# A hybrid encoder layer on one core: its interleaving planned with other durations, late issue of operations that wait for transfers, and the inverse's rows fetched by a transfer

## The chip, the cores and the metric

The kernel runs on one core of a Trainium2 chip. The metric is the device time of one execution in microseconds (us), a median of three runs; lower is better.

## What is computed

One layer over 1024 frames of width 1024, all in float32. Three groups of heads mix over time, a dense SwiGLU network follows, RMS norms stand before each and at the end:

```
h  = rmsnorm(x, ln1_g);  p = h @ w_in
ym = mlstm_group(pm, ...)     # 4 heads of 64, chunks of 64 frames in the reference
yr = retention_group(pr)      # 6 heads, chunkwise
yw = rwkv7_group(pw, ...)     # 6 heads, a recurrence per frame:
#   S = S * w_t - (S kk_t) (kk_t a_t)^T + v_t k_t^T ;  y_t = S r_t
x  = x + concat(ym, yr, yw) @ w_out
h  = rmsnorm(x, ln2_g)
x  = x + (silu(h @ w_gate) * (h @ w_up)) @ w_down       # D_FF 2816
return rmsnorm(x, lnf_g)
```

## The kernel before

Products of full precision are made of three products of rounded parts: each operand is split into a high part (`split_hi`, ScalarE, L90) and a low part (`split_lo`, VectorE, L93), and TensorE adds high x high, high x low and low x high. These triples are the dense work: L119 to L121 (512 columns), L729 to L731 (256 columns, token-major), L1171 to L1173 (first feed-forward layer), L1364 to L1366 (down-projection).

**The mixer** (up to some 760 us) is a set of generators, each a stream of its own: `rwkv_chain`, `rwkv_inverse`, the preparation of the RWKV heads, the output `rwkv_out`, `attention` (mLSTM and retention) and, last, `fillers` and `out_proj`, which bring the dense work. `weave` interleaves them as the program is written: it keeps a clock, each stream says with `yield cost, wait` how long its piece takes TensorE and how long its results take, and `yield "name"` waits for a `signal`. The stream whose time has come writes its next piece. Each engine executes its instructions in the order that comes out of this, and each engine waits at its own head. A stream that is in `sharing` holds the two accumulators until its tile is done.

**The RWKV recurrence** is taken in chunks of 64 frames. `rwkv_chain_pair` runs 16 steps, one after the other, for each of three pairs of heads, 48 in all. A step is: product of X and E (L581), copy to `pm` on ScalarE (L583), products L586 and L590, two copies to X on ScalarE (L592, L593), products L597 and L600, then the new state: X on VectorE (L607), its copy `st` on GpSimd (L609). Between these pieces `weave` puts pieces of other streams.

Each half of a pair needs the inverse of triangular matrices, six inverses in all (numbered 1 to 6 here). Gram products (L460) leave them in E; four small stores write them to `ab_d` in DRAM; one load brings them back as `MN`, each matrix in a partition, in four copies (L507). ScalarE copies the rows that each partition works on into `R` (L509, four copies). VectorE inverts by substitution in about 45 small operations (L514 to L522), GpSimd sets the diagonal of R (L527, four clearings to 1, the first of which needs only that R be there), R goes to `r_d` in DRAM and from there into E (L532). VectorE transposes a half of it (L535, tile `tq`), and two sets of small products on TensorE (L540, L546) complete the 64x64 inverse.

**Behind the mixer** `out_tile(1, d)` makes the second half of the output projection, in parts of six dense products; between parts, `between` steps `second_norm(0)`: `rms_stats` sums the squares (L159, of `sqa2`, which GpSimd has added up at L1049) and takes the root (L162), `rms_expand` spreads it over columns (L166). `second_half(d)` prepares operands on ScalarE, VectorE and GpSimd. Then comes the first feed-forward layer; its activations go to `a_dram` in DRAM, but for the tiles listed in `DIRECT`, which stay in SBUF. Before the down-projection `take` loads them back four tiles at a time (`rg`, two buffers) and splits them.

SyncE issues every transfer, in program order.

Of the kernel before, what the change touches and what calls it, by code (L numbers as in the profile page):

```python
# [19 lines left out]
P = 128  # L20
# [34 lines left out]
def trunk_kernel(ctx: ExitStack, tc: tile.TileContext, a: dict, out: bass.AP):  # L55
# [60 lines left out]
    def three(ps, w, xh, xl, ks=range(KT)):  # L116
        for k in ks:
# [3 lines left out]
            PE.matmul(ps, lhsT=lo, rhs=xh[:, k, :], start=False, stop=(k == KT - 1))  # L121
# [4 lines left out]
    clock, events = [0.0], {}  # L126
# [4 lines left out]
    def weave(gens, sharing):  # L131
        live = [[0.0, None, g] for g in gens + sharing]
        holder = None
        while live:
# [4 lines left out]
            got = next(s[2], None)  # L139
# [13 lines left out]
    PART = 6 * 0.214  # L153
# [36 lines left out]
    LAT = 0.93  # L190
    CHAIN, INV, ATT, NORM, MIX = 3.51, 20.16, 3.09, 3.26, 1.28
# [189 lines left out]
    def rwkv_half(i, h, r, k, v):  # L381
# [18 lines left out]
        yield 0.9, 3.0  # L400
# [32 lines left out]
        yield 2.6, 5.0  # L433
# [20 lines left out]
        yield 0.9, 5.5  # L454
# [20 lines left out]
        yield 3.4, 3.0  # L475
# [9 lines left out]
        yield 0.9, 1.0  # L485
# [14 lines left out]
    def rwkv_inverse():  # L500
        for i in range(3):
            for h in range(2):
# [5 lines left out]
                for g in range(4):  # L508
                    S.copy(out=R[lane(g)], in_=MN[lane(g), g::4, :])  # L509
                yield 0.0, 8.0  # L510
# [3 lines left out]
                V.tensor_tensor(tv, mf[:, 34:34 + 15 * 66:66].unsqueeze(2).broadcast_to([P, 15, 32]), MN[:, 2:31:2], ALU.mult)  # L514
# [18 lines left out]
                yield 0.0, 7.5  # L533
                for q in range(2):
                    V.transpose(out=T11[blk(q, 0)], in_=E[blk(q, 0), :, q, col(0)])  # L535
# [15 lines left out]
                yield 0.9, 3.0  # L551
# [5 lines left out]
    def rwkv_chain_pair(i):  # L557
        st = None
        for h in range(2):
# [3 lines left out]
            for c in range(8):  # L563
# [20 lines left out]
                yield 0.2, LAT  # L584
# [9 lines left out]
                yield 0.2, LAT  # L594
# [24 lines left out]
                yield 0.4, CHAIN  # L619
# [4 lines left out]
    def rwkv_out():  # L624
# [3 lines left out]
        for i in range(3):  # L628
            for h in range(2):
                yield f"prep{i}{h}"  # L630
                for b in range(2):
# [6 lines left out]
                    G.tensor_tensor(add, add, ga, ALU.mult)  # L638
# [11 lines left out]
                    signal(f"out{n}", 0.5)  # L650
                    V.tensor_tensor(gl, gl, pt, ALU.mult)
# [7 lines left out]
                    yield 0.9, 0.0  # L659
# [47 lines left out]
    def tok_proj(g, ts=range(KT)):  # L707
# [16 lines left out]
        for t in ts:  # L724
            ps = acc_tile()
            o = ps[:, 0:n]
            h, sl = chunk_of(t)
            for k in range(KT):
                PE.matmul(o, lhsT=xh[h][:, k, sl], rhs=w[k][0], start=(k == 0), stop=False)  # L729
                PE.matmul(o, lhsT=xh[h][:, k, sl], rhs=w[k][1], start=False, stop=False)  # L730
                PE.matmul(o, lhsT=xl[h][:, k, sl], rhs=w[k][0], start=False, stop=(k == KT - 1))  # L731
                if k == 3:
                    yield 12 * 0.42e-3 * n, 0.0, True
# [4 lines left out]
            elif g in (2, 3, 4):  # L738
                v4, o4 = (z.rearrange("p (h x d) -> p h x d", x=2, d=32) for z in (vt, o))
                cs = rot[:, t, :].rearrange("p (w x d) -> p w x d", w=2, x=2)  # L740
                b4 = etmp(256, "vb").rearrange("p (h x d) -> p h x d", x=2, d=32)
                V.scalar_tensor_tensor(vt.rearrange("p (h d) -> p h d", d=64), in0=o.rearrange("p (h d) -> p h d", d=64),
                                       scalar=rstd[:, t:t + 1], in1=rot[:, t:t + 1, 0:64].broadcast_to([P, 4, 64]),
# [17 lines left out]
            cost = 12 * 0.42e-3 * n  # L761
# [7 lines left out]

    rot = at.tile([P, KT, P], F32, name="rot", tag="rot")  # L770
    SY.dma_start(out=rot, in_=a["rot"])
# [360 lines left out]
    with ExitStack() as ph3:  # L1132
# [174 lines left out]
        def take(h, g, parts=None):  # L1307
# [6 lines left out]
            for f in range(gs.start, gs.stop, 4)[parts or slice(None)]:  # L1314
# [10 lines left out]
                for z in range(0, n, 2):  # L1325
# [3 lines left out]
                    for y in range(o, o + 2):  # L1329
                        ah[h, gs.start + y] = hi[:, y, :], lo[:, y, :]  # L1330
# [232 lines left out]
```

## Time and profile before

| | |
|---|---|
| runs | 1519.3, 1505.03, 1511.74 us; median 1511.74 |
| the profiled execution | 1521.67 us, span 1519.9 us, mean TensorE clock 0.952 |
| TensorE busy | 1425.6 us (94%), 8434 products |
| VectorE, ScalarE, GpSimd busy | 59%, 37%, 29% |
| transfers | 164.55 MB, 33.5% of 16 engines |
| chain that ended last | TensorE 53%, VectorE 3%, GpSimd 2%, transfers 2% |

The profile gives each instruction's start and length, the idle time of its engine before it, and behind an arrow what ended that idle time. The granted clock is a share of full speed. Products are pipelined, so the length of one (0.39 us for 512 columns) is more than the distance to the next.

### The profile page before, as it was taken

The page shows a single profiled execution, that of the slowest core. Times are in us where ns is not written, and L with a number is a line of the kernel's source. Part 1 is how long each engine was busy: PE and PEld are TensorE (multiplying, and loading weights), DVE is VectorE, ACT ScalarE, POOL GpSimd, SP SyncE. Part 2 cuts the span into 40 slices and gives each one's busy share as a digit, 9 for nine tenths or more (in the row PEclk, how much of TensorE's full clock was granted, in tenths as well). Part 3 has the DMA queues.
Part 4 walks back from the last instruction along what each step waited for, and adds up shares of the span by engine and source line. Part 5 has one row for each costly group of instructions (what it writes and reads, how often), then busy time and mean ns, then how long its engine had stood idle before and what let it go on. Part 6 is the DMA issues. An engine that isn't in the chain of part 4 may idle for free.

```text
span 1519.9 us, 23085 instructions
## 1 busy us (share of the span) xinstructions
PE 1425.6 (94%) x8434; PEld 1161.3 (76%) x8434; DVE 892.4 (59%) x1762; ACT 556.2 (37%) x1202; POOL 437.9 (29%) x539
## 2 busy tenths in 40 slices
PE   7998799789998998999998999999999998999996
PEld 5777577777777887887777887888888886887886
DVE  6457567458847756645468555555555565347434
ACT  6353334333432133244456333333333344224222
POOL 3211013234424333333545433344444420000000
PEclk9999999999978889899999999999999999999998
DMA  5142122334422244354632222222222247337333
GB/s 209 43 136 66 50 80 74 83 89 112 122 59 68 85 129 124 106 161 142 220 112 85 96 83 83 72 73 78 83 84 83 83 168 255 93 95 238 98 97 111
DMA packets 122269, 164.55 MB, mean 108 GB/s; under 512 B 38028, under 2 KB 70956, under 8 KB 120876
## 3 DMA queue, kind: packets, MB, share of 16 engines
q1 hardware_dynamic: 122156, 163.08, 33.5%
q8 instruction: 66, 1.08, 0.3%
q14 instruction: 47, 0.39, 0.1%
HBM read 124.75 MB, written 38.29 MB: 107 GB/s over the span
## 4 chain that ended last, share of the span: by engine, by line
PE 53%; DVE 3%; POOL 2%; DMA 2%; issue 1%; ACT 0%; POOLq 0%; DVEq 0%; SPq 0%; ACTq 0%
PE acc L1171 5%; PE acc L1172 5%; PE acc L1173 5%; PE chain L1365 5%; PE chain L1364 5%; PE chain L1366 5%; PE misc L1172 4%; PE misc L1171 4%; PE misc L1173 4%; PE acc L119 2%; PE acc L121 2%; PE acc L120 2%; DVE act L93 1%; PE acc L729 1%; PE acc L731 1%
## 5 line engine op out<-in xcount | busy, mean ns | idle before, releaser
L93 DVE TENSOR_TENSOR wlo<-wraw,whi 128x512 fp32r<-128x512 f32 (+1 forms) x210 | 147.9, 707 | 138.3 <-ACT whi L90 137.1
L90 ACT ACTIVATE whi<-wraw 128x512 fp32r<-128x512 f32 (+1 forms) x210 | 128.1, 612 | 226.3 <-PE chain L1365 117.9
L729 PE MATMUL acc<-whi,act 128*128 128x256 f32 (+1 forms) x512 | 161.3, 318 | 4.4 <-ACT whi L90 3.4
L90 ACT ACTIVATE whi<-rg 128x512 fp32r<-128x512 f32 x128 | 79.8, 631 | 228.7 <-POOL rg L1232 90.0
L730 PE MATMUL acc<-wlo,act 128*128 128x256 f32 (+1 forms) x512 | 155.4, 305 | 5.2 <-DVE wlo L93 5.2
L119 PE MATMUL acc<-act,whi 128*128 128x512 f32 x352 | 152.3, 433 | 7.0 <-ACT whi L90 6.2
L93 DVE TENSOR_TENSOR wlo<-rg,whi 128x512 fp32r<-128x512 f32 x128 | 93.1, 728 | 108.1 <-ACT whi L90 105.9
L731 PE MATMUL acc<-whi,act 128*128 128x256 f32 (+1 forms) x512 | 153.0, 300 | 0.0
L1364 PE MATMUL chain<-act,whi 128*128 128x512 f32 (+1 forms) x374 | 144.3, 386 | 4.0 <-ACT act L90 4.0
L120 PE MATMUL acc<-act,whi 128*128 128x512 f32 x352 | 145.5, 413 | 1.5 <-DVE act L252 1.5
L121 PE MATMUL acc<-act,wlo 128*128 128x512 f32 x352 | 145.7, 414 | 1.1 <-DVE wlo L93 1.1
L1365 PE MATMUL chain<-act,whi 128*128 128x512 f32 (+1 forms) x374 | 144.0, 385 | 0.5 <-DVE act L93 0.5
L1366 PE MATMUL chain<-act,wlo 128*128 128x512 f32 (+1 forms) x374 | 143.8, 384 | 0.0
L1171 PE MATMUL acc<-act,whi 128*128 128x512 f32 x352 | 139.3, 396 | 3.4 <-ACT pre L1432 2.7
L1173 PE MATMUL acc<-act,wlo 128*128 128x512 f32 x352 | 138.8, 394 | 0.0
L1172 PE MATMUL acc<-act,whi 128*128 128x512 f32 x352 | 138.5, 394 | 0.0
L729 PEld LDWEIGHTS acc<-whi,act 128*128 128x128 f32 x512 | 104.3, 205 | 12.1 <-ACT whi L90 3.9
L730 PEld LDWEIGHTS acc<-wlo,act 128*128 128x128 f32 x512 | 105.0, 206 | 9.2 <-DVE wlo L93 6.7
L731 PEld LDWEIGHTS acc<-whi,act 128*128 128x128 f32 x512 | 105.2, 206 | 1.0
L1172 PE MATMUL misc<-act,whi 128*128 128x512 f32 x264 | 104.1, 394 | 0.0
L1171 PE MATMUL misc<-act,whi 128*128 128x512 f32 x264 | 104.0, 394 | 0.0
L1173 PE MATMUL misc<-act,wlo 128*128 128x512 f32 x264 | 103.8, 393 | 0.0
(327 smaller groups left out, 2835.9 us busy)
## 6 DMA issues: line engine op xcount, KB each, us to landing
wraw<-in_w_down SPq DMA_DIRECT2D x85, 256.0 KB, 2.7
rg<-in_w_gate SPq DMA_DIRECT2D x22, 512.0 KB, 4.9
rg<-in_w_up SPq DMA_DIRECT2D x22, 512.0 KB, 5.0
a_dram<-work SPq DMA_DIRECT2D x41, 256.0 KB, 2.2
wraw<-in_w_tm SPq DMA_DIRECT2D x40, 256.0 KB, 3.0
rg<-a_dram SPq DMA_DIRECT2D x10, 1024.0 KB, 6.1
v_dram<-vt SPq DMA_DIRECT2D x64, 128.0 KB, 1.9
wraw<-in_w_out SPq DMA_DIRECT2D x32, 256.0 KB, 3.2
```

The source lines that it names most:

```text
L90: S.activation(hi, src, AF.Copy, scale=scale)
L93: (eng or V).tensor_tensor(lo, src, hi.bitcast(F32), ALU.subtract)
L119: PE.matmul(ps, lhsT=hi, rhs=xh[:, k, :], start=(k == 0), stop=False)
L729: PE.matmul(o, lhsT=xh[h][:, k, sl], rhs=w[k][0], start=(k == 0), stop=False)
L730: PE.matmul(o, lhsT=xh[h][:, k, sl], rhs=w[k][1], start=False, stop=False)
L731: PE.matmul(o, lhsT=xl[h][:, k, sl], rhs=w[k][0], start=False, stop=(k == KT - 1))
L1171: PE.matmul(ps, lhsT=hi, rhs=hi_x[:, k, :], start=(start and k == 0), stop=False, skip_group_check=True)
L1172: PE.matmul(ps, lhsT=hi, rhs=lo_x[:, k, :], start=False, stop=False, skip_group_check=True)
L1173: PE.matmul(ps, lhsT=lo, rhs=hi_x[:, k, :], start=False, stop=(stop and k == 3), skip_group_check=True)
L1364: PE.matmul(ps, lhsT=hi, rhs=hi_a[:, sl], start=(f == 0), stop=False)
L1365: PE.matmul(ps, lhsT=hi, rhs=lo_a[:, sl], start=False, stop=False)
L1366: PE.matmul(ps, lhsT=lo, rhs=hi_a[:, sl], start=False, stop=(f == FT - 1))
```

## The change

It has these parts:

- `weave` starts at 10.0 and uses other costs and waits throughout. The pieces of streams that do not share the accumulators are issued behind the last dense product written (`issue_after(dense[0])`).
- `late(eng)` issues an operation behind the last instruction that was written for its engine, wherever the scheduler would have put it. It is used for the inverse's first operation and its transposes, GpSimd's product in `rwkv_out`, the split of `yw`, and the mLSTM weights, which are now made in a function of their own.
- R is loaded from `ab_d` by a transfer of 1024 rows of 128 bytes, behind that of MN; the four copies are gone.
- The rotary table, one load of 512 KB before, is loaded in 24 tiles of 64 KB, two buffers, where it is used.
- `second_norm` sums three parts later for the first half, and four parts, not two, lie between sum and expansion. `second_half(7)` is issued behind ScalarE's first copy to `pre`.
- Four tiles of activations stay in SBUF, not two, and the load of tiles 16 to 19 brings only the two that do not.

```diff
-    clock, events = [0.0], {}
+    clock, events = [10.0], {}
+    def late(eng):
+        return tc.issue_after(next(i for i in reversed(nc.cur_bb.bb.instructions) if i.engine == eng.engine))
+    dense = [None]
...
-            got = next(s[2], None)
+            with nullcontext() if s[2] in sharing or dense[0] is None else tc.issue_after(dense[0]):
+                got = next(s[2], None)
...
-    PART = 6 * 0.214
+    PART, TOK = 6 * 0.23, 12 * 0.47e-3
-    LAT = 0.93
-    CHAIN, INV, ATT, NORM, MIX = 3.51, 20.16, 3.09, 3.26, 1.28
+    LAT, CHAIN, INV, ATT, NORM, MIX = (1.2, 1.6), 3.4, 28.0, 4.0, 4.0, 1.6
...
                 SY.dma_start(out=MN, in_=ab_d.rearrange("b q c s t -> (b q c) (s t)").unsqueeze(0).broadcast_to([4, 32, 1024]))
-                for g in range(4):
-                    S.copy(out=R[lane(g)], in_=MN[lane(g), g::4, :])
-                yield 0.0, 8.0
+                SY.dma_start(out=R, in_=ab_d.rearrange("b q c (j g) t -> g (b q c) j t", g=4))
+                yield 0.0, 11.0
...
-                V.tensor_tensor(tv, mf[:, 34:34 + 15 * 66:66].unsqueeze(2).broadcast_to([P, 15, 32]), MN[:, 2:31:2], ALU.mult)
+                with late(V):
+                    V.tensor_tensor(tv, mf[:, 34:34 + 15 * 66:66].unsqueeze(2).broadcast_to([P, 15, 32]), MN[:, 2:31:2], ALU.mult)
...
-                yield 0.0, 7.5
+                yield 0.0, 9.0
                 for q in range(2):
-                    V.transpose(out=T11[blk(q, 0)], in_=E[blk(q, 0), :, q, col(0)])
+                    with late(V):
+                        V.transpose(out=T11[blk(q, 0)], in_=E[blk(q, 0), :, q, col(0)])
...
                 S.copy(out=pm, in_=chn[:, 0:64])
-                yield 0.2, LAT
+                yield 0.4, LAT[0]
...
                 S.copy(out=X[64:128, c, 1, :], in_=chn[64:128, 64:128])
-                yield 0.2, LAT
+                yield 0.45, LAT[1]
...
-                    G.tensor_tensor(add, add, ga, ALU.mult)
...
                     signal(f"out{n}", 0.5)
+                    with late(G):
+                        G.tensor_tensor(add, add, ga, ALU.mult)
...
+            if g in (2, 3, 4):
+                rot = at.tile([P, P], F32, name="rot", tag="rot", bufs=2)
+                SY.dma_start(out=rot, in_=a["rot"][:, t, :])
...
-                cost = 12 * 0.42e-3 * n
+                cost = TOK * n
...
-    rot = at.tile([P, KT, P], F32, name="rot", tag="rot")
-    SY.dma_start(out=rot, in_=a["rot"])
...
+    def mlstm_weights(c, ws):
+        for q, w in enumerate(ws):
...
+                yield 0.0, 3.0
+                with late(S):
+                    split_hi(yh[:, 5 + i], yw)
...
         rms_stats(const, [sqa2[h]], 4, f"b{h}", rs)
-        yield
-        yield
+        for _ in range(4):
+            yield
...
-        DIRECT = (FT - 2, FT - 1)
+        DIRECT = range(FT - 4, FT)
...
-                n = min(4, gs.stop - f)
+                here = [y for y in range(f, min(f + 4, gs.stop)) if h == 0 and y in DIRECT]
+                n = min(4, gs.stop - f) - len(here)
...
-        between = chain(second_norm(0), first_half())
+        between = chain(second_norm(0, 4), first_half())
...
-        second_half(KT - 1)
...
-                S.copy(out=pre[j, m], in_=ps[m])
+                copy = S.copy(out=pre[j, m], in_=ps[m])
+                if j == m == 0:
+                    with tc.issue_after(copy.ins):
+                        second_half(KT - 1)
```

What this does to the order of instructions is shown at three places; the line numbers of the new kernel differ from those of the old.

On VectorE, around the start of inverse 6 in the kernel before (`rt<-MN` is the inverse's first operation, `X<-st,dl,chain` the chain's new state, `vt` and `wlo` belong to the dense streams):

```order
L758 SCALAR_TENSOR_TENSOR vt<-acc,rstd_x,vt 128x256
L514 TENSOR_TENSOR rt<-MN 128x480
L515 TENSOR_TENSOR MN<-MN,rt 128x15x32
L519 TENSOR_TENSOR rt<-R,MN 128x60
L758 SCALAR_TENSOR_TENSOR vt<-acc,rstd_x,vt 128x256
L522 TENSOR_TENSOR R<-R,rt 128x30
L93 TENSOR_TENSOR wlo<-wraw,whi 128x512
L522 TENSOR_TENSOR R<-R,rt 128x30
L607 SCALAR_TENSOR_TENSOR X<-st,dl,chain 64x64
```

The same place in the changed kernel:

```order
L762 TENSOR_TENSOR vt<-acc,rdec 128x256
L520 TENSOR_TENSOR rt<-MN 128x480
L93 TENSOR_TENSOR wlo<-wraw,whi 128x512
L521 TENSOR_TENSOR MN<-MN,rt 128x15x32
L614 SCALAR_TENSOR_TENSOR X<-st,dl,chain 64x64
L525 TENSOR_TENSOR rt<-R,MN 128x60
L614 SCALAR_TENSOR_TENSOR X<-st,dl,chain 64x64
L528 TENSOR_TENSOR R<-R,rt 128x30
```

The first half of X stands three instructions behind the first operation on MN, where it stood seven behind, and the second half stands behind the first operation that reads R.

On ScalarE at the same inverse, in the kernel before (`pm` and `X` are the chain's copies):

```order
L583 COPY pm<-chain 128x64
L509 COPY R<-MN 32x256 x4
L755 ACTIVATE vt<-acc,rhalf 128x256
L592 COPY X<-chain 64x64
L593 COPY X<-chain 64x64
```

In the changed kernel, with tile numbers, at the step of the chain that follows inverse 6's Gram products:

```order
L590 COPY pm_6579<-chain_6578 128x64
L90 ACTIVATE whi_6765<-wraw_6747 128x512
L90 ACTIVATE whi_6773<-wraw_6749 128x512
L599 COPY X_4912<-chain_6578 64x64
L600 COPY X_4912<-chain_6578 64x64
```

The four copies of R stood between the chain's copies; nothing of the inverse stands there now.

On TensorE where the token-major tiles of `fillers` end and the output projection begins, in the changed kernel (L588 to L607 are a chain step, L547 and L553 the two sets of products of inverse 6, L953 a transpose of the retention, L119 to L121 and L742 dense products; `E_6203` is the tile whose inverse is number 6):

```order
L742 MATMUL acc_7223<-whi_7082,act_109 128x256
L588 MATMUL chain_7292<-X_4912,E_5055 64x64 x2
L119 MATMUL acc_7527<-act_6245,whi_7519 128x512
L120 MATMUL acc_7527<-act_6246,whi_7519 128x512
L121 MATMUL acc_7527<-act_6245,wlo_7520 128x512
L593 MATMUL chain_7292<-pm_7293,E_5055 64x64 x2
L597 MATMUL chain_7292<-st_7203,E_5055 64x64 x2
...
L604 MATMUL chain_7292<-X_4912,E_5055 64x64 x2
...
L547 MATMUL misc_7255<-tq_7122,E_6203 32x32 x15
...
L588 MATMUL chain_7379<-X_6089,E_6203 64x64 x2
L121 MATMUL acc_7527<-act_6245,wlo_7520 128x512
L553 MATMUL misc_7255<-E_6203,tq_7123 32x32 x16
```

In the kernel before, the second set of inverse 6 and the first step that uses that inverse stand there (L729 and L731 are token-major dense products):

```order
L546 MATMUL misc_6889<-E_5951,tq_6670 32x32 x16
...
L731 MATMUL acc_7006<-whi_6778,act_109 128x256
L581 MATMUL chain_7021<-X_5793,E_5951 64x64 x2
L729 MATMUL acc_7006<-whi_6786,act_108 128x256
L730 MATMUL acc_7006<-wlo_6787,act_108 128x256
L731 MATMUL acc_7006<-whi_6786,act_109 128x256
```

The last eight steps of the chain and the end of inverse 6 stood among the token-major tiles, 26 rows apart; they now begin where these tiles end, side by side.

More of the change, by code (lines that the diff above doesn't have):

```diff
@@ L1 @@
 import math
-from contextlib import ExitStack
+from contextlib import ExitStack, nullcontext
 from itertools import chain
@@ L730, in tok_proj @@
                 PE.matmul(o, lhsT=xh[h][:, k, sl], rhs=w[k][1], start=False, stop=False)
[L731 removed]
+                dense[0] = PE.matmul(o, lhsT=xl[h][:, k, sl], rhs=w[k][0], start=False, stop=(k == KT - 1)).ins
                 if k == 3:
[L733 removed]
+                    yield TOK * n, 0.0, True
             vt = etmp(256, "vt")
@@ L1098, in attention, with weigh @@
     def attention():
-        mlstm = ("mlstm", 2.6, mlstm_load, mlstm_chunk, mlstm_finish, None)
-        ret = ("ret", 4.0, ret_load, ret_chunk, ret_finish, ret_store)
+        def weigh(t, args):
+            if len(args) == 4:
+                with late(G):
+                    mlstm_weights(t, args[-1])
+        mlstm = ("mlstm", 4.2, mlstm_load, mlstm_chunk, mlstm_finish, None)
+        ret = ("ret", 5.0, ret_load, ret_chunk, ret_finish, ret_store)
         for (name, cost, load, chunk, finish, store), start, ts in (
@@ L1106, in attention @@
             yield 0.0, 6.0
+            weigh(ts.start, args)
+            yield 0.0, 2.0
             for t in ts:
@@ L1314, in take @@
             for f in range(gs.start, gs.stop, 4)[parts or slice(None)]:
-                n = min(4, gs.stop - f)
-                if h == 0 and f in DIRECT:
-                    for y in range(f, f + n):
-                        o = y - gs.start
-                        split_hi(hi[:, o, :], direct[y])
-                        split_lo(lo[:, o, :], direct[y], hi[:, o, :])
-                        ah[h, y] = hi[:, o, :], lo[:, o, :]
-                    continue
-                r = sb.tile([P, 4, HF], F32, name="rg", tag="rg", bufs=2)
-                SY.dma_start(out=r[:, 0:n, :], in_=a_dram[h][:, f:f + n, :])
-                for z in range(0, n, 2):
-                    o = f - gs.start + z
-                    split_hi(hi[:, o:o + 2, :], r[:, z:z + 2, :])
-                    split_lo(lo[:, o:o + 2, :], r[:, z:z + 2, :], hi[:, o:o + 2, :])
-                    for y in range(o, o + 2):
-                        ah[h, gs.start + y] = hi[:, y, :], lo[:, y, :]
+                here = [y for y in range(f, min(f + 4, gs.stop)) if h == 0 and y in DIRECT]
+                n = min(4, gs.stop - f) - len(here)
+                if n:
+                    r = sb.tile([P, 4, HF], F32, name="rg", tag="rg", bufs=2)
+                    SY.dma_start(out=r[:, 0:n, :], in_=a_dram[h][:, f:f + n, :])
+                parts = [(f + z, 2, r[:, z:z + 2, :]) for z in range(0, n, 2)] + [(y, 1, direct[y].unsqueeze(1)) for y in here]
+                for y, m, src in parts:
+                    o = slice(y - gs.start, y - gs.start + m)
+                    split_hi(hi[:, o, :], src)
+                    split_lo(lo[:, o, :], src, hi[:, o, :])
+                    for z in range(m):
+                        ah[h, y + z] = hi[:, o.start + z, :], lo[:, o.start + z, :]
         x3 = {}
```

29 lines of the change are left out of this document (15 added, 14 removed).

## The prediction

> **What bounds the kernel now.** I read the page's first, second and fourth parts, then stretches of the span, then what TensorE waited for.
>
> ```profile
> PE 1425.6 (94%) x8434; PEld 1161.3 (76%) x8434; DVE 892.4 (59%) x1762; ACT 556.2 (37%) x1202; POOL 437.9 (29%) x539
> PE 53%; DVE 3%; POOL 2%; DMA 2%; issue 1%; ACT 0%; POOLq 0%; DVEq 0%; SPq 0%; ACTq 0%
> 0.00:750.00 750.00, 681.55 (x5172) 557.56 (x5173) 473.90 (x1178) 283.78 (x750) 230.48 (x396) 0.92 0.34 106
> 750.00:820.00 70.00, 64.56 (x274) 52.16 (x274) 50.30 (x59) 39.54 (x67) 38.19 (x26) 0.95 0.42 140
> 820.00:1240.00 420.00, 416.55 (x1802) 336.61 (x1802) 232.91 (x320) 143.50 (x247) 162.62 (x114) 1.00 0.24 83
> 1240.00:1265.00 25.00, 20.50 (x81) 15.86 (x80) 18.99 (x24) 12.38 (x17) 3.77 (x2) 0.89 0.72 253
> ```
>
> In the stretches the first number after the bounds is the length, the second TensorE's busy time, and the number third from the end the granted clock. TensorE bounds the whole, but not evenly. From 820 to 1240 us it is busy for 416.55 of 420 us at full clock: nothing is to be had there, and 416.55 / 1802 gives the price of a dense product of 512 columns, 0.23 us. Up to 750 us, the mixer, it stands idle for 750 - 681.55 = 68 us, and a mean clock of 0.92 costs another 0.08 x 750 = 60 us. The change works on this stretch, on the 70 us behind it (5.4 us idle, 3.5 us of clock) and on the start of the down-projection (4.5 us idle, 0.11 x 25 = 2.8 us of clock). That is some 145 us that an edit of the order can reach at all. The waits name the places:
>
> ```profile
> PE misc L540 <- DVE tq L535: 10.5, 3, 7.7
> PE chain L597 <- ACT X L593: 7.8, 3, 6.0
> PE chain L586 <- ACT pm L583: 7.6, 5, 2.0
> PE chain L1364 <- ACT act L90: 4.0, 1, 4.0
> PE misc L159 <- POOL sqa L1049: 3.8, 1, 3.8
> PE acc L729 <- ACT whi L90: 3.4, 2, 3.0
> PE acc L1171 <- ACT pre L1432: 2.7, 2, 1.6
> PE misc L166 <- POOL rs L162: 1.6, 1, 1.6
> ```
>
> (Total, times, longest.) The waits put down to ScalarE, `ACT`, come from no slow ScalarE, as the longest of them shows, first in order of time and then as two stretches:
>
> ```profile
> 584.40 0.53 SPq L507 DMA_DIRECT2D MN<-ab_d  x1
> 588.49 0.33 PE L586 MATMUL chain<-pm,E 64*64 64x64 f32 x4
> 594.03 1.65 ACT L509 COPY R<-MN 32x256 f32<-32x256 f32 x4 [6.80 <-DMA MN<-ab_d]
> 594.03 0.66 DVE L514 TENSOR_TENSOR rt<-MN 128x480 f32<-128x480 f32 x1 [5.89 <-DMA MN<-ab_d]
> 596.08 0.19 ACT L592 COPY X<-chain 64x64 f32<-64x64 f32 x1
> 596.56 0.48 PE L597 MATMUL chain<-X,E 128*64 128x64 f32 x4 [6.02 <-ACT X L593]
> 590.20:593.70 3.50, 0.34 (x3) 0.14 (x2) 0.00 (x0) 0.00 (x0) 0.00 (x0) 1.00 0.22 71
> 593.70:600.50 6.80, 3.94 (x23) 3.83 (x24) 5.29 (x15) 4.93 (x14) 1.52 (x4) 0.50 0.18 60
> ```
>
> The inverse's copy out of MN stands at the head of ScalarE's queue 6.80 us before MN lands; the chain's copy of X, whose input was there from 588.8 us, stands behind it, and TensorE in its own queue behind that. Then the clock falls to 0.50 for 6.8 us, which costs 3.4 us more. So a stall of 6 us costs 9.4.
>
> **The change part by part.** *R by transfer, the inverse's first operation and transposes later.* Six times four copies leave ScalarE; nothing of the inverse then waits for MN there. The stalls behind such a copy are the three of L597 (7.8), the longest of L586 (2.0) and of L729 (3.0): 12.8 us. The 7.69 us of L540 are the same thing on VectorE:
>
> ```profile
> 161.24 0.66 DVE L514 TENSOR_TENSOR rt<-MN 128x480 f32<-128x480 f32 x1 [7.81 <-DMA E<-r_d]
> 162.54 0.44 DVE L535 STREAM_TRANSPOSE tq<-E 32x256 f32<-32x256 f32 x1
> 163.12 0.28 PE L540 MATMUL misc<-tq,E 32*32 32x32 f32 x2 [7.69 <-DVE tq L535]
> ```
>
> The first inverse's transposes stand behind the second's first operation, which waits for MN. In the new order the pair of transposes stands ahead of it. Together 20.5 us at most. I leave 3 us for what follows: the wait for MN stays on VectorE, and now the chain's X update stands two or three rows behind it, its second half behind the first reader of R. MN landed 9.6 us after its issue above; the wait of 5.89 began 10.6 us behind the last Gram product at 577.5. In the new order the operation stands one third farther behind the Gram products (9.9 against 7.1 us, an estimate: the rows between, at 0.23 us for a dense product), so about 3 us of wait stay, and the next product that needs X has a chain's pause of 18 dense products, 4.1 us, to cover them. Term: **-17** (0 to -20).
>
> New there is the transfer of R, in 1024 rows of 128 bytes. Not seen; its nearest rows are the store of R with the same rows, and a plain store of the same size:
>
> ```profile
> 634.70 4.89 DMA r_d<-R
> v_dram<-vt SPq DMA_DIRECT2D x64, 128.0 KB, 1.9
> 639.65 2.06 DMA E<-r_d
> 641.74 0.45 DVE tq L535
> 642.24 0.31 PE misc L540 x2
> ```
>
> Issued right behind MN it lands with MN (0) or 4.9 us behind it; the first two operations on MN take 1.3 us, so 0 to 3.6 us more of wait in each of inverses 3 to 6, 0 to 14 us. I take nearly 0, since it moves beside the 512 KB of MN, and keep the end for the range. [...]
>
> *Clock.* Behind the other stalls that go (those at 155, 300 and 488 us) lie low stretches too:
>
> ```profile
> 160.20:167.00 6.80, 3.88 (x23) 2.71 (x25) 3.42 (x6) 2.33 (x5) 0.17 (x2) 0.50 0.16 51
> 307.00:313.80 6.80, 6.20 (x29) 5.86 (x30) 4.23 (x13) 1.30 (x5) 0.41 (x1) 0.50 0.56 170
> 491.30:501.50 10.20, 10.02 (x53) 8.58 (x54) 6.45 (x19) 3.06 (x12) 3.60 (x5) 0.50 0.37 122
> ```
>
> With the one shown above they are 6.8 + 6.8 + 10.2 + 6.8 = 30.6 us at half clock, 15 us lost. Half of them I let return elsewhere, since the mixer's thin stretches stay thin: **-8** (0 to -15).
>
> *Norm sums later.* rms_stats stands 3 parts later, and two more parts lie between it and the expansion, by the code; a part is six products.
>
> ```profile
> 763.38 1.68 POOL sqa L1049
> 765.10 1.87 PE misc L159 x8
> 1251.48 7.88 DMA rg<-a_dram
> 1260.49 0.80 PE L1364 MATMUL chain<-act,whi 128*128 128x512 f32 x1 [4.04 <-ACT act L90]
> rg<-in_w_gate SPq DMA_DIRECT2D x22, 512.0 KB, 4.9
> ```
>
> GpSimd's last addition of squares ends at 765.06, 3.79 us after TensorE came to its sum. A part is 6 x 0.23 = 1.4 us, so three parts cover 4.1 us. The 1.6 of L166 get 2.8 us more cover, and the 2.7 of L1171 go because second_half(7) is issued behind the copy that they wait for. 8.1 us idle, 3.4 us of clock; I keep 2.5 us for what is then late: **-9** (-3 to -11).
>
> *Last activations from SBUF.* The load that lands at 1259.36 shrinks from 1024 to 512 KB: by the row of that size 4.9 instead of 7.88 us, so TensorE's 4.04 become about 1, and half of the stretch's 2.8 us of clock: **-4** (0 to -7).
>
> *New costs.* A chain step keeps 6 dense products ahead of L586 and gets 12 instead of 6 ahead of L597: 48 steps x 6 x 0.23 = 66 us of cover more, and the last step stands 24 us of TensorE's work later (estimated from the order, as above). So when the dense fillers end, nine steps stand before it and not five, among thin retention products. A thin stretch of today:
>
> ```profile
> 416.40:419.80 3.40, 2.62 (x26) 2.28 (x26) 2.58 (x8) 0.82 (x2) 2.69 (x5) 0.98 0.22 34
> 419.80:423.20 3.40, 3.40 (x13) 2.29 (x12) 1.25 (x5) 0.41 (x2) 0.00 (x0) 0.50 0.35 66
> ```
>
> Four steps more at half a microsecond each, and one low stretch of 6.8 us or more: **+6** (0 to +25). [...]
>
> The GpSimd product behind the transposes, the split of yw and the mLSTM weights issued later I cost at 0: GpSimd (29%) and ScalarE (37%) have the room, and what each then waits for has landed. The 24 transfers of rot wait for one of two tiles, which VectorE frees two column tiles earlier; behind them in SyncE's queue stand the other loads, MN too. As long as VectorE is less than two tiles late (a tile is 24 products of half the columns, so 2 x 12 x 0.23 = 5.5 us) they cost nothing; if it is later, MN is as late, and that is the first rival.
>
> Sum: -17 - 8 - 9 - 4 + 6 = **-32 us**. The profiled execution took 1521.67 us, span 1519.9, and would come to 1490. It lies 10 us above the median of 1511.74; from the median, which the comparison will use, it is **1480**.
>
> **Rivals.** *The wait only changes engines.* MN, and R up to 4.9 us later, still hold VectorE, and the first clearing of R holds GpSimd until R lands; the chain's X and state copies stand behind both. For it: 5.89 us of L514 in the same row as the copies. Against it: the cover above. The first two terms then give nothing, the rest -7 to -13: about **1500**.
>
> *The inverse becomes the bound: slower.* L540 stands in TensorE's queue with every stream behind it. From MN to the stored R inverse 6 took 634.70 - 594.03 = 40.7 us, then 7 us of transfers; stalls of TensorE hid some of that. With those gone, the new order gives 44.5 us from its Gram products to L540 (38.7 before, the same estimate) against 64.7 measured, and the chain's second half starts right there, where before it stood 26 rows behind. If inverses 2 to 6 were each late by 5 us, with 3.4 us of clock each, 42 us would go: 1480 + 42 = **1522**. It decides from 3 us a time (5 x 6.4 = 32). For it speaks that L540 waited in three of six already; against it that VectorE, busy for 59%, catches up when TensorE slows.
>
> *The clock comes back wholly.* If the thin windows fall below what the clock needs only because of the stalls, the other half of the second term and some 15 us of the 60 return: about **1457**.
>
> **How the numbers follow.** Forecast 0.52 (its own range 1465 to 1497), wait on another engine 0.22, inverse as the bound 0.15, clock back 0.11. A measurement of this kernel tells about 1% from no change: faster means below 1496.6, slower above 1526.9. Most of the forecast, all of the last rival and a third of the first give 0.68 faster; same gets 0.22, slower 0.10. The range, 1452 to 1514, leaves out the worst of the inverse rival and the top of the last one.
>
> **What would show it.** Right: no L509-like copies, no wait of over 3 us of L597 or L586 for ScalarE, no 7 us in front of L540, L159 below 1 us, the down-projection's wait near 1 us, a clock of 0.94 or more up to the end of the mixer. Wrong: L540 waiting for tq in all inverses, L581 for X, or a low clock where the fillers end.

## The result, and the profile after

The changed kernel takes 1500.11 us (median of ten runs, 1492.21 to 1505.56) against 1518.13 for ten runs of the kernel before: the medians lie 18 us apart, and the ratio is 0.9873, 95% interval 0.9852 to 0.9893. The prediction said -32 us, 1480 with a range of 1452 to 1514. The profiled execution took 1500.5 us, span 1498.7.

The first lines of its page (busy times, chain), then stretches of the span as in the prediction:

```profile
PE 1418.3 (95%) x8434; PEld 1152.0 (77%) x8434; DVE 885.4 (59%) x1763; ACT 547.5 (37%) x1179; POOL 436.2 (29%) x539
PE 71%; DVE 8%; DMA 8%; issue 3%; POOL 2%; ACT 2%; SPq 1%; DVEq 0%; POOLq 0%; ACTq 0%
0.00:750.00 750.00, 692.49 (x5257) 561.74 (x5258) 475.91 (x1196) 285.94 (x746) 232.83 (x399) 0.94 0.37 110
650.00:700.00 50.00, 49.97 (x411) 39.34 (x411) 24.93 (x57) 20.14 (x61) 17.90 (x23) 0.90 0.45 144
750.00:800.00 50.00, 44.58 (x185) 35.23 (x183) 39.63 (x40) 25.72 (x44) 31.35 (x21) 0.93 0.45 155
800.00:1230.00 430.00, 428.89 (x1848) 348.11 (x1849) 241.73 (x331) 150.96 (x258) 168.74 (x117) 0.99 0.23 82
1230.00:1265.00 35.00, 30.79 (x123) 24.24 (x122) 19.35 (x26) 16.02 (x25) 0.45 (x1) 0.90 0.81 277
```

Up to 750 us TensorE now idles 57.5 us, not 68, and the clock is 0.94, not 0.92. Behind that little moved. What TensorE waited for (total, times, longest), with the old names L540, L597, L586, L581, L1364 and L1171 in the same roles as L547, L604, L593, L588, L1382 and L1193; `mq` holds queries and keys of the mLSTM, `rsw` is a tile of the retention, `yw` the output of the recurrence. The last two rows are VectorE's, in the changed kernel and in the kernel before:

```profile
PE acc L119 <- ACT whi L90: 8.4, 2, 5.8
PE chain L604 <- ACT X L600: 6.4, 4, 5.3
PE misc L547 <- DVE tq L542: 3.9, 2, 3.1
PE misc L977 <- DVE rsw L967: 3.9, 2, 2.4
PE misc L412 <- DVE gate L659: 3.8, 1, 3.8
PE chain L1382 <- ACT act L90: 3.7, 1, 3.7
PE chain L588 <- DVE X L614: 3.7, 3, 2.6
PE misc L887 <- DMA mq<-mqk_dram: 2.9, 1, 2.9
PE acc L1193 <- ACT pre L1449: 2.8, 1, 2.8
PE misc L655 <- POOL yw L851: 2.5, 1, 2.5
PE chain L593 <- ACT pm L590: 1.2, 2, 0.7
DVE rt L520 <- DMA MN<-ab_d: 12.5, 4, 4.5
DVE rt L514 <- DMA MN<-ab_d: 10.2, 3, 5.9
```

ScalarE no longer stands for MN. VectorE does in both kernels, and less than before: to the 10.2 us of the last row belong two more stands at the same operation, 7.8 and 4.8 us, that the profile puts down to other transfers, 22.8 us in all. In the changed kernel the four waits are 4.5, 2.0, 3.2 and 2.7 us, the 3 us or so a time that the prediction worked out.

The 5.8 us in the first row are the start of the program, which the kernel before has too (6.2).

One account helps with all runs below. From each trace I took TensorE's idle time, and half of the time that it worked at half clock (granted clock 0.50) as "lost to the clock". Idle time is counted between the first and the last product; the 6 us before and the 7 us after them are left in the rest, and the half clock in those 7 us (some 3.5 us in every run) is counted as lost. What is left of the span is nearly the same in all fourteen profiles, 1371 to 1380 us: the work itself. So, but for these 9 us, the differences are idle time and clock.

| kernel (label) | median us | ratio to before, 95% | span | idle | lost to clock | rest |
|---|---|---|---|---|---|---|
| before | 1518.13 | | 1519.9 | 80.9 | 65.2 | 1373.8 |
| changed | 1500.11 | 0.9873 (0.9852 to 0.9893) | 1498.7 | 67.5 | 55.5 | 1375.8 |
| tail_only | 1511.9 | 0.9984 (0.9956 to 1.0013) | 1510.3 | 73.3 | 60.5 | 1376.5 |
| mixer_only | 1500.14 | 0.9913 (0.9884 to 0.9941) | 1498.8 | 62.3 | 56.4 | 1380.0 |
| r_by_dma | 1522.06 | 1.0046 (1.0016 to 1.0077) | 1526.3 | 85.0 | 70.6 | 1370.7 |
| r_copies | 1510.02 | 0.9966 (0.9939 to 0.9994) | 1517.2 | 78.4 | 67.2 | 1371.6 |
| old_numbers | 1520.6 | 1.0036 (1.0016 to 1.0057) | 1512.1 | 68.6 | 68.7 | 1374.8 |
| wait_old | 1532.62 | 1.0082 (1.0053 to 1.0112) | 1533.3 | 89.1 | 67.6 | 1376.5 |
| lat_old | 1516.57 | 0.9984 (0.9956 to 1.0012) | 1513.5 | 81.5 | 57.1 | 1374.8 |
| no_late | 1486.65 | 0.9813 (0.9791 to 0.9836) | 1491.2 | 66.2 | 50.3 | 1374.8 |
| weights_back | 1511.24 | 0.9965 (0.9939 to 0.9991) | 1497.3 | 67.6 | 55.9 | 1373.7 |
| exps_late | 1493.88 | 0.9837 (0.9811 to 0.9862) | 1494.9 | 63.8 | 52.3 | 1378.8 |
| early_load | 1495.45 | 0.9878 (0.9852 to 0.9903) | 1492.8 | 65.9 | 52.0 | 1375.0 |
| tail_order | 1488.22 | 0.9832 (0.9803 to 0.9861) | 1479.5 | 62.2 | 38.4 | 1378.9 |

The ratio compares with runs of the kernel before that were taken on the same chip (medians from 1516.0 to 1518.7) and is what the text goes by; it is not the plain quotient of the medians and differs from it by up to 0.25 points (mixer_only: 0.9888). One profile can lie 10 us and more from its kernel's median (weights_back: 1499 against 1511). Every edit of the mixer lets the whole order come out anew, so a difference between two of these kernels is that of two orders.

### The profile page after: what moved, and what is told of

Same layout as the page of the kernel before. It is cut to its first block, busy times and chain, and to the rows that moved or that the text cites. A ratio compares the mean times of both kernels' runs of the same rounds, so it can differ in the third digit from the quotient of the medians.

```text
span 1498.7 us, 23112 instructions
## 1 busy us (share of the span) xinstructions
PE 1418.3 (95%) x8434; PEld 1152.0 (77%) x8434; DVE 885.4 (59%) x1763; ACT 547.5 (37%) x1179; POOL 436.2 (29%) x539
## 4 chain that ended last, share of the span: by engine, by line
PE 71%; DVE 8%; DMA 8%; issue 3%; POOL 2%; ACT 2%; SPq 1%; DVEq 0%; POOLq 0%; ACTq 0%
PE acc L1193 5%; PE acc L1195 5%; PE acc L1194 5%; PE chain L1383 5%; PE chain L1382 5%; PE chain L1384 5%; PE acc L119 4%; PE misc L1193 4%; PE misc L1195 4%; PE misc L1194 4%; PE acc L121 4%; PE acc L120 3%; PE acc L740 2%; PE acc L741 2%; PE acc L742 2%
## 5 line engine op out<-in xcount | busy, mean ns | idle before, releaser
L119 PE MATMUL acc<-act,whi 128*128 128x512 f32 x352 | 152.3, 433 | 8.6 <-ACT whi L90 8.4
L740 PE MATMUL acc<-whi,act 128*128 128x256 f32 (+1 forms) x512 | 153.5, 304 | 4.4 <-ACT whi L90 3.9
L741 PE MATMUL acc<-wlo,act 128*128 128x256 f32 (+1 forms) x512 | 151.4, 296 | 3.3 <-DVE wlo L93 3.3
L121 PE MATMUL acc<-act,wlo 128*128 128x512 f32 x352 | 146.5, 417 | 2.9 <-DVE wlo L93 2.9
L742 PE MATMUL acc<-whi,act 128*128 128x256 f32 (+1 forms) x512 | 149.3, 292 | 0.0
L1382 PE MATMUL chain<-act,whi 128*128 128x512 f32 (+1 forms) x374 | 144.3, 386 | 3.7 <-ACT act L90 3.7
L1193 PE MATMUL acc<-act,whi 128*128 128x512 f32 x352 | 140.1, 398 | 2.8 <-ACT pre L1449 2.8
L740 PEld LDWEIGHTS acc<-whi,act 128*128 128x128 f32 x512 | 99.1, 195 | 10.9 <-ACT whi L90 4.7
L741 PEld LDWEIGHTS acc<-wlo,act 128*128 128x128 f32 x512 | 100.1, 195 | 8.4 <-DVE wlo L93 4.5
L1193 PE MATMUL misc<-act,whi 128*128 128x512 f32 x264 | 104.2, 395 | 0.0
L742 PEld LDWEIGHTS acc<-whi,act 128*128 128x128 f32 x512 | 100.0, 195 | 1.6 <-issue 0.3
```

The source lines that it names most:

```text
L119: PE.matmul(ps, lhsT=hi, rhs=xh[:, k, :], start=(k == 0), stop=False)
L742: dense[0] = PE.matmul(o, lhsT=xl[h][:, k, sl], rhs=w[k][0], start=False, stop=(k == KT - 1)).ins
L1193: PE.matmul(ps, lhsT=hi, rhs=hi_x[:, k, :], start=(start and k == 0), stop=False, skip_group_check=True)
L1382: PE.matmul(ps, lhsT=hi, rhs=hi_a[:, sl], start=(f == 0), stop=False)
```

## The edits behind the mixer, and the mixer alone

`tail_only` is the kernel before with `second_norm(0, 4)`, the two further yields, `second_half(KT - 1)` behind the first copy to `pre`, and four tiles in `DIRECT`. `mixer_only` is the changed kernel with these undone.

```diff
-        DIRECT = (FT - 2, FT - 1)
+        DIRECT = range(FT - 4, FT)
...
-        between = chain(second_norm(0), first_half())
+        between = chain(second_norm(0, 4), first_half())
```

> The kernel before with the edits behind the mixer alone: norm sums later, second_half(7) behind the first copy to pre, four activation tiles kept in SBUF. My prediction gave these -13 us. Reading the two traces: idle time from 750 us to the down-projection's start fell only from 13.4 to 10.7 us and the clock lost more than before. By that theory the run lies within 4 us of the kernel before (1518); if the prediction's terms were right, near 1505.

> The changed kernel with those same edits undone: the mixer alone is changed. If the whole gain is the mixer's, as the traces say, it takes about the changed kernel's time (1497 to 1503); if the edits behind the mixer earn their 13 us, about 1513.

Measured: 0.9984 and 0.9913. The edits behind the mixer bring between -7 and +2 us by their interval, not the -13 of the prediction, and the changed kernel without them has most of the gain: its median is that of the changed kernel, its ratio 0.4 points worse, and the two intervals overlap. The timelines say why. First, the norm sums, in the changed kernel and, in the last line, in `mixer_only`:

```profile
757.77 0.72 ACT L1063 ACTIVATE x<-x,vec 128x512 f32<-128x512 f32 x1 [2.94 <-DMA x_dram<-x]
760.96 0.60 PE L119 MATMUL acc<-act,whi 128*128 128x512 f32 x1 [2.58 <-ACT whi L90]
763.15 0.79 PE L121 MATMUL acc<-act,wlo 128*128 128x512 f32 x1 [1.16 <-DVE wlo L93]
801.11 0.50 PE L1193 MATMUL acc<-act,whi 128*128 128x512 f32 x1 [2.79 <-ACT pre L1449]
757.65 0.50 PE L119 MATMUL acc<-act,whi 128*128 128x512 f32 x1 [2.02 <-ACT whi L90]
```

TensorE's 3.79 us before the sum of squares are gone, in `tail_only` too (where 2.3 us stand before the expansion instead of 1.6). But they are also gone in `mixer_only`, which sums as early as the kernel before: in the new order of the mixer this wait is not there to be saved. What stands at this place with the new mixer is another wait, with the later sums (2.58 + 1.16 us) and without them (2.02 + 0.59): before ScalarE can scale x in place, it stands for x to be stored, 2.94 us in the changed kernel, and the next weights' split stands behind that. The first copy to `pre`, moved ahead of second_half(7), still has two splits of the last operands and a square ahead of it: 2.79 us, where two waits made 2.7 before (4.16 in `mixer_only`).

Second, the down-projection (the load is from the chain of work, the rest from the timeline):

```profile
1228.32 0.39 PE L1382 MATMUL chain<-act,whi 128*128 128x512 f32 x1
1231.89 7.49 DMA rg<-a_dram
1239.40 2.95 ACT L90 ACTIVATE act<-rg 128x1024 fp32r<-128x1024 f32 x3 [2.53 <-DMA rg<-a_dram]
1240.51 0.79 PE L1382 MATMUL chain<-act,whi 128*128 128x512 f32 x1 [3.74 <-ACT act L90]
```

From its first product at 1228.32 to the wait's beginning at 1236.77 TensorE works 8.45 us and makes 36 products: twelve activation tiles. What it then waits for is tile 12, from the load of tiles 12 to 15, which still has 1024 KB. The load that the change shrinks brings tiles 16 and 17, which come later. The same count fits the kernel before (1247.97 to 1256.45). I had taken one load for the other.

Two runs were built on this. `early_load` takes tiles 16 and 17 into two buffers of their own, and was still written under the wrong reading:

```diff
...
+                if i == last - 4:
+                    for y in (FT - 6, FT - 5):
+                        direct[y] = sb.tile([P, HF], F32, name="pre", tag="pre", bufs=2 * NPRE)
+                        SY.dma_start(out=direct[y], in_=a_dram[0][:, y, :])
```

> The changed kernel with the two activation tiles that the shrunken load brings loaded into two free buffers of their own, about an item and a half earlier, so that the load no longer waits for VectorE to free a buffer of rg. Theory: the 3.7 us before the down-projection's 13th product stayed because the load still starts when that buffer is free and then takes 7.5 us among the other transfers, whatever its size; with its own buffer the wait falls under 1 us, and the 3.4 us of clock behind it go too: -3 to -7 us. Rival: the splits on ScalarE and VectorE are late by then (they finish at 1236 now): -1 to 0.

Measured: 0.9878, and the wait stays, 3.68 us; its theory fell. `tail_order` (on top of it, and of `no_late` below) lets the first column tile of the down-projection take tiles 16 to 21 before 12 to 15:

```diff
+            order = (0, 4, 8, 16, 20, 12) if h == d == 0 else tuple(range(0, FT, 4))
...
```

> The changed kernel without late issue on VectorE, and with the down-projection's first tile taken in another order: the activation tiles 16 and 17, loaded early into two free buffers, and 18 to 21, which stay in SBUF, come before tiles 12 to 15, whose load of 1024 KB is what TensorE waits for. The mixer is that of the run without late issue. Theory: the 3.7 us in front of the 13th group of products go, since six tiles x 3 products x 0.23 = 4.2 us of work stand there instead, and with them up to 3.4 us of clock: 3 to 7 us below the run without late issue, about 1481 (0.976 to 0.980 of before). Rival: the splits of those six tiles on ScalarE and VectorE are not done by then, and another wait of 2 to 4 us takes the place: no change.

Measured: 0.9832, no better than `no_late` (0.9813). The wait for tile 12 is gone; in its place, from this run's timeline:

```profile
1222.50 2.01 ACT L90 ACTIVATE act<-rg 128x1024 fp32r<-128x1024 f32 x2 [1.51 <-DMA rg<-a_dram]
1223.09 0.51 PE L1388 MATMUL chain<-act,wlo 128*128 128x512 f32 x1 [3.97 <-DVE wlo L93]
```

The rival came true: with the tiles there, VectorE, which has all the low parts to make at this place, is late with those of the weights.

## R by transfer: nothing alone, much with the new waits

`r_by_dma` is the kernel before with this edit alone; `r_copies` is the changed kernel with the four copies back.

```diff
-                for g in range(4):
-                    S.copy(out=R[lane(g)], in_=MN[lane(g), g::4, :])
+                SY.dma_start(out=R, in_=ab_d.rearrange("b q c (j g) t -> g (b q c) j t", g=4))
```

> The kernel before with one edit: R by a transfer in place of ScalarE's four copies. Theory: ScalarE's stand at MN was what held the chain; L597 and L586 no longer wait for ScalarE over 1 us, the waits of 6.0, 3.0 and 2.0 go and some clock with them: -8 to -15 us. Rival, the wait only changes engines: VectorE stands for MN and R, L581 or L597 waits for it, 0 to -4 us. The 7.7 us before L540 stay in both.

> The changed kernel with R copied by ScalarE again, in place of the transfer. Theory (of the prediction): ScalarE then stands at MN in front of the chain's copies, some 2 to 5 us each time as the first operation on VectorE does now, +4 to +10 us. Rival, after the transfer alone gave nothing in the kernel before: the chain is held by VectorE at MN anyway, and R by transfer comes 1 to 2 us later than MN; then -4 to +3 us.

Measured: alone it makes the kernel 0.2 to 0.8% slower, so that the theory of a gain fell, and the rival of none was still too good; taken out of the changed kernel it costs 0.9% (0.9966 against 0.9873), as the theory had it and at the upper end or above. The place at 590 us in `r_by_dma`, to be read beside the timeline in the prediction (its line numbers are one lower):

```profile
589.89 0.21 ACT L592 COPY X<-chain 64x64 f32<-64x64 f32 x1
594.84 0.66 DVE L513 TENSOR_TENSOR rt<-MN 128x480 f32<-128x480 f32 x1 [6.06 <-DMA MN<-ab_d]
597.14 0.22 DVE L518 TENSOR_TENSOR rt<-R,MN 128x60 f32<-128x60 f32 x1 [0.96 <-DMA R<-ab_d]
599.24 0.27 DVE L606 SCALAR_TENSOR_TENSOR X<-st,dl,chain 64x64 f32<-64x64 f32 x1
599.57 0.98 PE L580 MATMUL chain<-X,E 128*64 128x64 f32 x4 [5.72 <-DVE X L606]
```

ScalarE is free and copies X at once (589.89; 596.08 before). Half a step later the chain needs its new state from VectorE, and that stands behind the same MN, then behind R: 5.72 us for 6.02. The wait changed engines, as my first rival said. The longest wait of this run stands elsewhere, though:

```profile
303.67 0.40 ACT L862 ACTIVATE w<-w,gtok 128x128 f32<-128x128 f32 x1 [9.27 <-POOL w L859]
306.28 0.48 PE L596 MATMUL chain<-X,E 128*64 128x64 f32 x4 [8.59 <-ACT X L592]
```

Here ScalarE is not free: it stands for weights of the mLSTM, for whose load GpSimd waits 6.67 us, and the chain's copies stand behind. In the kernel before four waits around this place made 6.0 us.

The transfer of R also has a price that neither the prediction nor these theories had. In the changed kernel at inverse 4:

```profile
385.72 0.56 SPq L514 DMA_DIRECT2D R<-ab_d  x1
388.71 6.75 SPq L936 DMA_DIRECT2D ym_dram<-hh  x1
395.51 1.16 SPq L860 DMA_DIRECT2D mq<-mqk_dram  x2
398.61 0.71 PE L887 MATMUL misc<-mq 64*128 64x128 f32 x8 [2.91 <-DMA mq<-mqk_dram]
```

An issue takes SyncE 0.34 us in the median of the changed kernel. The one right behind R's takes 3.7 to 9.6 us in the changed kernel, at all six inverses, and 3.4 to 10.9 us in all eleven kernels with this transfer, with one exception among 66; in the three kernels without it no issue takes over 3.4 us. (One other issue of the changed kernel takes as long, `w<-g_d`, 5.89 us at 263.76.) Whatever stands behind it in SyncE's queue is held back with it: here two loads of `mq`, for which TensorE then waits 2.91 us. Nine of the eleven kernels with the transfer have a wait for `mq`, none of the three without. What this costs elsewhere was not measured.

In the changed kernel VectorE reaches MN later (it stands there 12.5 us in all, 22.8 before); with the copies back ScalarE is again the engine that holds the chain, with waits of 12.2 us for X (6.4 in the changed kernel) and 8.3 for pm (1.2).

## The numbers

`old_numbers` is the changed kernel with all the old costs and waits, `wait_old` with three of them, `lat_old` with the chain's own.

```diff
-                yield 0.0, 11.0
+                yield 0.0, 8.0
...
-                yield 0.0, 9.0
+                yield 0.0, 7.5
...
-    LAT, CHAIN, INV, ATT, NORM, MIX = (1.2, 1.6), 3.4, 28.0, 4.0, 4.0, 1.6
+    LAT, CHAIN, INV, ATT, NORM, MIX = (1.2, 1.6), 3.4, 20.16, 4.0, 4.0, 1.6
```

(That is `wait_old`; `lat_old` has LAT (0.93, 0.93), chain costs 0.2, 0.2 and 0.4, CHAIN 3.51.)

> The changed kernel with all the planner's costs and waits of the kernel before (clock from 0, parts at 0.214, LAT 0.93, INV 20.16, waits of 8.0 and 7.5 around the transfers, and so on), everything else as changed. Theory now: the gain of the mixer comes from the distances that the numbers make, since a transfer of R alone gave nothing. Then this run is at 1513 to 1522, with waits of 4 us and more of TensorE for X or tq where MN or E lands. Rival: the late issue and the pieces placed behind dense products bring it; then 1500 to 1506.

> The changed kernel with three numbers of before: 8.0 us of plan between the load of MN and the inverse's first operation (for 11.0), 7.5 from the store of R to its transposes (for 9.0), 20.16 for the inverse on VectorE (for 28.0). Theory: these distances carry most of what all old numbers cost, since MN lands 9 us after its issue whatever the plan says: +8 to +18 us, with waits of 4 us or more of TensorE for X or tq. Rival: the chain's own covers carry it; then within 5 us.

> The changed kernel with the chain's numbers of before: waits of 0.93 us behind both of its copies, costs of 0.2, 0.2 and 0.4 and 3.51 between steps. Theory: the many short waits for pm (7.6 us in five before, 1.2 in two after) come back and with them low-clock stretches: +4 to +10 us. Rival: the distances around the transfers carry the gain, and this stays within 4 us, or gains by the shorter chain (-2 to -5).

Measured: 1.0036, 1.0082 and 0.9984. With the old numbers nothing is left of the gain, although R comes by transfer and the late issue is there. The three waits alone cost 2.1 points of the ratio (0.9873 to 1.0082), more than they were expected to, and more than all the old numbers together: the costs of single numbers do not add up, so no share of the gain can be given to one of them. Their waits, TensorE's and then VectorE's at inverse 5:

```profile
PE misc L547 <- DVE tq L542: 13.2, 3, 8.1
PE acc L740 <- DVE R L528: 11.0, 2, 6.8
PE chain L593 <- ACT pm L590: 9.7, 4, 8.1
504.88 0.66 DVE L520 TENSOR_TENSOR rt<-MN 128x480 f32<-128x480 f32 x1 [9.15 <-DMA MN<-ab_d]
507.65 0.55 PE L740 MATMUL acc<-whi,act 128*128 128x256 f32 x1 [4.18 <-DVE R L528]
```

VectorE stands 9.15 us for MN, and even dense products wait. Behind it stand VectorE's reads of the accumulators (L753 and L757; the last ends at 507.50, and the next tile's first product starts at 507.65) and the low parts of weights, for which TensorE waits 1.56 us more at 509.76. The chain's numbers cost 1.1 points, some 16 us and more than the theory's 4 to 10, and not by the waits named there: pm stays at 1.4 us in all; instead dense products wait 15.7 us for ScalarE's high parts of weights. Why these are late there was not followed up.

## Late issue on VectorE, and the mLSTM weights

`no_late` takes `late(V)` away from the inverse's first operation and its transposes.

```diff
-                with late(V):
+                with nullcontext():
...
-                    with late(V):
+                    with nullcontext():
```

> The changed kernel without late issue of the inverse's first operation and its transposes on VectorE (the other late issues stay). Theory: late issue is what puts the transposes of inverse 1 ahead of inverse 2's wait for MN; without it a wait of some 7 us for tq near 155 comes back with 3.4 us of clock, and VectorE stands earlier for MN elsewhere: +6 to +12 us against the changed kernel (1506 to 1512). Rival: the longer waits in the plan put them there anyway: within 4 us.

Measured: 0.9813, faster than the changed kernel by 0.6 points; the intervals do not touch. Both the theory and its rival fell. The wait for tq near 160 us does come back (4.5 and 1.4 us), and three others go: those for X at 415 (2.6), for tq at 440 (3.1) and for mq at 396 (2.9). But others come in their place, so that the idle time is nearly the same (66.2 against 67.5 us); what is gained in the profile is mostly clock, 50.3 us lost against 55.5. Why the clock is better in this order is not shown. How the wait for tq at 440 came about can be read in the changed kernel:

```profile
434.75 0.56 SPq L534 DMA_DIRECT2D r_d<-R  x1
439.58 1.81 SPq L538 DMA_DIRECT2D E<-r_d  x4
440.05 0.69 DVE L728 TENSOR_REDUCE wmean<-wraw 128x8 f32<-128x512 f32 x1 [5.40 <-DMA wraw<-in_w_tm]
442.20 0.43 DVE L542 STREAM_TRANSPOSE tq<-E 32x256 f32<-32x256 f32 x1
442.78 0.22 PE L547 MATMUL misc<-tq,E 32*32 32x32 f32 x2 [3.11 <-DVE tq L542]
```

VectorE stood 5.40 us for a load of weights, with the chain's X and the transposes written behind it. But that is not what made the wait. The store of R went out at 434.75, and the transposes came 7.45 us later; at inverse 6 of the kernel before, with VectorE free and waiting for E alone, the same way took 7.04 us (634.70 to 641.74, in the prediction's rows). TensorE had come to the products at 439.67. So nearly all of the 3.11 us are R's way through DRAM, and VectorE's stand adds some 0.4: the inverse was late here, once, as the prediction's second rival had feared for all. That the order without late issue is better as a rule is not shown; it is one order of this program.

The other stall that was new in the changed kernel stands at 299 us:

```profile
302.79 1.29 ACT L876 ACTIVATE w<-w,gtok 128x128 f32<-128x128 f32 x4 [6.07 <-POOL w L873]
303.99 0.19 ACT L599 COPY X<-chain 64x64 f32<-64x64 f32 x1
304.45 0.48 PE L604 MATMUL chain<-X,E 128*64 128x64 f32 x4 [5.33 <-ACT X L600]
```

ScalarE stands at the mLSTM weights' exponentials, which wait for GpSimd, with the chain's copies behind. Two runs asked whether that is the cost of this part: `weights_back` makes the weights in the load again, `exps_late` leaves GpSimd's addition where it is and issues the exponentials only at the head of the chunk:

```diff
...
             for t in ts:
+                exps(t, args)
                 y = chunk(t, *args)
```

> The changed kernel with the mLSTM weights made in the load again, as before. Theory: in the changed kernel ScalarE stands at the exponentials of the weights (6.07 us at 302, 3.61 us at 415), behind which the chain's copies and, through the norm's squares, its X on VectorE wait; with the weights back these two stalls (5.33 and 2.60 us) and some half clock go, -6 to -10 us. Rival: they wait in the load just as well, GpSimd then standing for the transfer of w, and the time stays (within 4 us) or gets worse.

> The changed kernel with the exponentials of the mLSTM weights taken out of the late piece and issued late on ScalarE only at the head of the chunk that uses them; GpSimd's addition stays where the change put it. Theory: ScalarE's stand at these exponentials (6.07 us at 302) is what holds the chain's copies there and gives the 5.33 us before L604; it goes, and with it 3 us of clock: -4 to -9 us. Rival, after putting the weights back into the load only moved the wait: the exponentials are needed by the chunk's own products soon after, and VectorE and TensorE then wait for them (L898 for w): within 4 us.

Measured: 0.9965 and 0.9837. Putting the weights back loses most of the gain, so in this order the late issue of the weights is worth having, against my theory. Where the time goes is not shown: the profile is of the fastest of twelve runs and has the changed kernel's idle time and clock (67.6 and 55.9 us). Issuing the exponentials later gains 0.4 points, with an interval (0.9811 to 0.9862) that overlaps that of the changed kernel (0.9852 to 0.9893), so the gain is not certain. But its profile shows the rival:

```profile
299.15 0.21 ACT L599 COPY X<-chain 64x64 f32<-64x64 f32 x1 [1.84 <-PE chain L597]
303.45 1.29 ACT L879 ACTIVATE w<-w,gtok 128x128 f32<-128x128 f32 x4 [3.87 <-POOL w L873]
307.29 1.11 PE L901 MATMUL misc<-MV,w 128*128 128x65 f32 x4 [6.64 <-DVE w L893]
```

The chain's copy is on time; then TensorE waits 6.64 us for the weights themselves. GpSimd makes them too late for this chunk in either order (it adds to them from 302.06 us on in the changed kernel, from 302.73 here). What was gained came elsewhere: the wait for X at 415 is gone, and the clock lost 3 us less.

## Why the prediction was right, and where it was not

- **The number**: in part luck. 1500.11 lies within the wide range, but outside the forecast's own range (1465 to 1497), and not below 1496.6, the "faster" to which the prediction gave 0.68. It is the time of the first rival, by coincidence: that rival lets the mixer's first two terms give nothing and keeps the edits behind the mixer, and the opposite was measured. Without the two terms behind the mixer the sum is -19, near the 18 us measured, but through errors that offset each other: idle time fell by less than forecast, the clock came back by more. The base was also low: 1511.74 from three runs, 1518.13 from ten.
- **What bounds the kernel**: right. Idle time and clock in the mixer were what moved: up to 750 us idle time fell by 11 us and the clock's loss by 12. Over the whole, idle -13.4, clock -9.7 and work +2 make the -21 us of the two spans.
- **First term, -17**: measured -11 of idle up to 750 us. The wait for tq at 155 fell from 7.69 to 0.79 us, those at 488 and 590 went, and the many short waits for pm, of which I had let all but the longest stand, fell from 7.6 to 1.2. Given back were 5.33 us at 299 for the mLSTM weights, costed at 0, 3.8 us at 253, where VectorE stands for a load of the mLSTM's gates, 2.6 and 3.1 us in front of X and tq, and 2.9 us for a load behind R's transfer. The cause was misplaced as well: the transfer of R, to which this term gave the stalls on ScalarE, is worth nothing without the longer waits (1.0046 alone). And the 7.69 us were not the order on VectorE alone: in the kernel before, the third of E's four loads, which the second transposes read, landed only at 162.30 by the trace. In the changed kernel R was stored 3 us earlier (145.54 against 148.54), and TensorE came to these products 2 us later (157.5 against 155.4).
- **R's arrival**: between the two ends. R was there 2.1 us after MN at inverse 3 (293.09 and 295.22) and 2.2 at inverse 4; VectorE waited 0.8 us at most for it. At inverse 3 R, a quarter of the bytes (128 KB for 512), was issued 0.6 us later than MN and landed 2.1 us later. This did not decide. What the term left out is SyncE, which the issue behind R's holds for 3.7 to 9.6 us.
- **Clock, -8**: measured -12 up to 750 us, what the new costs took already in it, and -9.7 in all.
- **Norm sums, -9, and last activations, -4**: these steps failed. Measured together -7 to +2 us on the old mixer. The first counted on a wait that is not there with the new mixer, and left out the wait for ScalarE that stands at the same place; the second shrank a load that TensorE does not wait for there.
- **New costs, +6**: smaller. The clock is 0.90 from 650 to 700 us, where the dense fillers end, but 0.93 from 600 to 650 where it was 0.81: from 600 to 750 us the clock costs 10 us in both kernels. New there is a wait of 2.5 us for yw at 740. The waits for the retention (1.5 and 2.4 us, at 565 and 603) stand among the token-major tiles.
- **Rivals**: the wait that changes engines is what the transfer alone does. The inverse did not become the bound: L547 waits 3.9 us in all. Of some 30 us of clock that the last rival counts on, 12 came back up to 750 us (17 with the half clock of idle time counted too); how much work in a stretch the clock needs, as that rival takes it, no run shows.
- **The signs**: no 7 us in front of the transposes' products, no wait for the sum of squares and a clock of 0.94 came true. A wait of 5.33 us for ScalarE's X, though not for MN, and the down-projection's 3.7 us spoke against the prediction, and so did the low clock where the fillers end.

## What to carry to other kernels

When an in-order engine stands at a transfer, look at which other engines stand at the same transfer before moving the work off the first: freeing one can move the wait to the next, as here from ScalarE (6.02 us) to VectorE (5.72 us); in this kernel the gain came only together with more distance to the transfer (1.0046 for the transfer alone; in the changed kernel 1.0036 with the old distances, 0.9873 with the new). Look at the issuing queue too: here the issue behind the load of 1024 rows of 128 bytes took SyncE 3.4 to 10.9 us, in 65 cases of 66. Before a gain is booked for an edit in one stage, ask whether the wait survives the edits in the stage before; a run with each half of the change alone shows it. Before a wait is put down to a load, count the products from the stage's start to the wait; the count names the tile. Take apart span, idle time and clock in each profile, and trust a difference of under 1% only from several runs.

## What was not expected of the hardware

The work left after idle time and clock stayed within 1371 to 1380 us over fourteen orders of the program, so no order made the products themselves dearer by more than these 9 us. The time at half clock ranged from 82 to 158 us at idle times of 62 to 89 us, and followed the idle time only loosely: old_numbers idled 68.6 us and lost 68.7 to the clock, the changed kernel 67.5 and 55.5. What else sets it stays open. Nor was it expected that the issue behind a load of 1024 rows of 128 bytes takes SyncE up to 10.9 us, where 0.34 is the median.
